# Block sums of the second feed-forward weights: from accumulating DMAs into SBUF at their use to sums made in DRAM during the attention stages

## The chip, the cores and the metric

The kernel runs on one core of one Trainium2 chip. The metric is the device time of one execution in microseconds; the kernel before has a median of 865.25 us in 3 runs (865.21 to 866.35). Engine names are those of the profile: PE is the matrix engine (PEld its weight loads), DVE VectorE, ACT ScalarE, POOL GpSimd, SP SyncE. DMAs issued by SyncE go to hardware queue q1, those of ScalarE to q10, those of GpSimd to the software queue q0; all three are served by the core's 16 DMA engines.

## The reference

One encoder layer on 512 rows of width 1024, in float32: a row norm, one wide projection, three attention branches (a gated linear attention, "GLA"; a softmax attention with forget gates, "FoX"; a cross attention into 256 memory rows), a gated merge with an output projection, and a feed-forward layer with squared ReLU. The part that the change touches:

```python
u2 = rmsnorm(h, g_ffn[l])
h = h + jnp.square(jax.nn.relu(u2 @ w_ff1[l])) @ w_ff2[l]
return rmsnorm(h, g_final)
```

w_ff1 is 1024 x 4096, w_ff2 4096 x 1024.

## The kernel before

All matrix products on weights are made of three products of a high and a low part (hi x hi, lo x hi, hi x lo; `mm3`, lines 122 to 125), so each weight chunk of 128 x 1024 float32 (512 KiB) that arrives from DRAM is split into two: ScalarE casts the high part, VectorE subtracts (`split_w`, lines 112 to 117, and `split`, lines 174 to 176). All weights lie in one DRAM array `wst`, laid out chunk by chunk in the order of use (`chunk_list`). `load_w` (line 109) issues a chunk's load on SyncE into one of three buffers "raw"; its two halves go into one of three buffers "hi" and "lo". So at most three chunks are split ahead of PE and three more loaded ahead of that.

The order of the program is: the front (memory keys and values, the row norms, u); chunk "G" (the low-rank and forget projections), the first fq and fk chunk, four fv chunks, the second fq and fk chunk; then three weaves, in which `weave` (line 160) takes attention steps from a list and puts chunks of projections between them by a count of units: the FoX heads (24 steps, with the gk, gq, fq, fk, gv and gg chunks between), the memory attention (16 steps) and the GLA (20 steps). After them come the last branch, the output projection, and the feed-forward layer.

PE's instructions stand in the order of the source. Those of the other engines, SyncE's and GpSimd's among them, are ordered by a scheduler when the program is built; the order on each engine is then fixed, and an instruction that waits holds up all behind it on its engine.

The feed-forward layer works on four quarters q of the inner width. For each, eight chunks of w_ff1 give the squared activations, and `second(q)` (line 950) multiplies by the quarter's part of w_ff2 by Strassen's scheme in the Winograd form: seven products n of half-size blocks in place of eight. The weights' blocks "11", "21", "12", "22" (two chunks i of 512 KiB each, one after the other in `wst`) are laid out such that the four sums which the scheme needs are plain sums: n = 5 uses 11+12, n = 6 11+12+22, n = 7 12+22, n = 4 the sum of all four. The kernel before loads the eight chunks of a quarter into eight buffers of their own by SyncE (line 954), and makes a sum in place by an accumulating DMA on GpSimd's queue, which adds another chunk from DRAM to the buffer (`factor`, line 961): 8 per quarter, 32 in all. Each chunk of a factor is then split (`split_b`), and 12 products follow.

Of the kernel before, what the change touches and what calls it, by code (L numbers as in the profile page):

```python
# [9 lines left out]
F32 = mybir.dt.float32  # L10
# [4 lines left out]
ALU = mybir.AluOpType  # L15
AX = mybir.AxisListType

P = 128
# [43 lines left out]
def hybrid_block(ctx, tc, chunks, wst, xT, memT, xN, cols, gffn, gfin, wup, cst, out):  # L62
    nc = tc.nc
    PSUM = bass.MemoryType.PSUM
    index = {c: i for i, c in enumerate(chunks)}
# [3 lines left out]
    def nm(s):  # L69
        uid[0] += 1  # L70
        return f"{s}_{uid[0]}"
# [5 lines left out]
    dram = ctx.enter_context(tc.tile_pool(name="dram", bufs=1, space=bass.MemoryType.DRAM))  # L77
# [4 lines left out]
    def mmt(shape=None):  # L82
        return pmm.tile(shape or [P, 512], F32, tag="mm", name=nm("mm"))

    def at_(shape=None):
        return pa.tile(shape or [P, 512], F32, tag="a", name=nm("a"))
# [35 lines left out]
    def mm3(ps, lh, ll, rh, rl, start, stop):  # L122
        nc.tensor.matmul(ps, lh, rh, start=start, stop=False)  # L123
        nc.tensor.matmul(ps, lh, rl, start=False, stop=False)  # L124
        nc.tensor.matmul(ps, ll, rh, start=False, stop=stop)  # L125
# [29 lines left out]
    def run(*gens):  # L155
        for g in gens:
            for _ in g:
                pass

    def weave(steps, units, *gens):  # L160

        fill = chain(*gens)
        done = 0
        for i, st in enumerate(steps):
            st()
            due = units * (i + 1) // len(steps)
            while done < due and next(fill, fill) is not fill:
                done += 1
        run(fill)
# [4 lines left out]
    def split(hi, lo, src):  # L174
        nc.scalar.copy(hi, src)  # L175
        return nc.vector.tensor_tensor(lo, src, f(hi), op=ALU.subtract).ins  # L176
# [174 lines left out]
    with pool("fox") as xp:  # L351
# [176 lines left out]
        for h in range(10):  # L528
            for fn, i in ((fox_values, h - 2), (fox_turn, h - 1), (fox_scores, h)):
                if 0 <= i < 8:  # L530
                    steps.append(partial(fn, i))
        weave(steps, 128, gla_k(0), gla_k(1), gla_q(0), gla_q(1), fox_pair(2), fox_pair(3), gvg,
              *[gla_g(j) for j in range(4)])

# [44 lines left out]
    with pool("mematt") as ap:  # L579
# [52 lines left out]
        for h in range(6):  # L632
            for fn, i in ((mem_values, h - 2), (mem_turn, h - 1), (lambda i: run(mem_q(i)), h + 1), (mem_scores, h)):
                if 0 <= i < 4:
                    steps.append(partial(fn, i))
        weave(steps, 96, branch("gate_fox", "w_fox_o", ofh, ofl, 0))
    kvst.close()
    ofst.close()


    with pool("gla") as lp:
# [5 lines left out]
        for e in range(2):  # L647
            b = slice(64 - 64 * e, 128 - 64 * e)
# [108 lines left out]
        def idle(_):  # L757
# [4 lines left out]
            (decays, 1), (gla_turn, 0), (gla_turn, 1), (key_turn, 1), (gla_scores, 2), (states, 1), (gla_scores, 3),  # L762
            (gla_values, 2), (gla_values, 3), (gla_turn, 2), (gla_turn, 3))]
        weave(steps, 96, branch("gate_mem", "w_mem_o", omh, oml, 1))
    gst.close()
    omst.close()
# [94 lines left out]
    with pool("ff") as yp:  # L861
# [8 lines left out]
        def split_b(raw):  # L870
            split_n[0] += 1
            own = split_n[0] % 4 == 0
            hi, lo = ((yp if own else wp).tile([P, 1024], F32R, tag=g, name=nm(g), bufs=1 if own else 3)
                      for g in (("bhi", "blo") if own else ("hi", "lo")))
            split(hi, lo, raw)
            return [t.rearrange("p (k c) -> p k c", k=2) for t in (hi, lo)]
# [39 lines left out]
        def evac(q, n, t, ps):  # L916
            last = q == NQ - 1
            if n == 1 and last:
                add(C(0, 0, t), ps)
            if n in (6, 7):  # L920
                R = (R6 if n == 6 else R7)[t]
                if q == 0:
                    nc.scalar.copy(R, ps)
                else:
                    add(R, ps)
            if n == 6 and last:
                E, G = R6[t], scratch()
                nc.vector.tensor_tensor(E, held[1][t], R6[t], op=ALU.subtract)
                nc.vector.tensor_tensor(G, held[5][t], E, op=ALU.subtract)
                add(C(1, 0, t), E)  # L930
                add(C(1, 1, t), G)
                add(C(0, 1, t), G)
            if n == 7 and last:
                add(C(1, 1, t), R7[t], ALU.subtract)
                finish(2 + t, 1, 0)
                add(C(1, 0, t), R7[t])
            if n == 4:
                add(C(1, 0, t), ps)
                if last:
                    finish(2 + t, 0, 1)  # L940
            if n == 3:
                add(C(0, 1, t), ps)
                if last:
                    finish(t, 1, 1)
            if n == 2:
                add(C(0, 0, t), ps)
                if last:
                    finish(t, 0, 0)

        def second(q):  # L950
            raw = {(b, i): yp.tile([P, 1024], F32, tag=f"b{b}{i}", name=nm("raw")) for b in ("11", "21", "12", "22")
                   for i in range(2)}
            for (b, i), t in raw.items():
                nc.sync.dma_start(t, wst[index["B", q, i, b]])

            def factor(n, i):

                to, x = {1: ("11", None), 5: ("11", "12"), 6: ("11", "22"), 7: ("12", "22"), 4: ("11", "21"), 3: ("22", None),
                         2: ("21", None)}[n]
                if x is not None:  # L960
                    nc.gpsimd.dma_start(raw[to, i], wst[index["B", q, i, x]], accum_op=ALU.add)  # L961
                return split_b(raw[to, i])

            for n, slot in ((1, 0), (2, 1), (5, 3), (6, 4), (7, 5), (4, 2), (3, 6)):
                keep = n in (1, 5)
                if not keep:
                    ps = [mmt() for _ in range(2)]
                else:
                    ps = held.setdefault(n, [at_() for _ in range(2)] if q == 0 else None)
                end = q == NQ - 1 and n == 3  # L970
                steps = [[0, 1]] if end else [[0], [1]]
                for js in steps:
                    w = {i: factor(n, i) for i in js}
                    for t in range(2):
                        for i in js:
                            for k in range(2):
                                p = 2 * i + k
                                sl = slice(t * P, (t + 1) * P)
                                mm3(ps[t], A[p][0][:, slot, sl], A[p][1][:, slot, sl], w[i][0][:, k, :], w[i][1][:, k, :],
                                    p == 0 and not (keep and q), p == 3 and (not keep or q == NQ - 1))  # L980
                        if js[-1] == 1 and not (keep and q < NQ - 1):
                            evac(q, n, t, ps[t])

        for q in range(NQ):
            A.clear()
            for j in range(8):
                if q == 0 and j < 2:
                    act_evac(first[j])
                    continue
                key = ("T", "w_ff1", P * (8 * q + j))  # L990
                if q == 0 and j < 4:
                    with tc.issue_after(norm_end):
                        w = get_w(key)
                else:
                    w = get_w(key)
                run(gT(w, u2h, u2l, act_evac))
            if q == NQ - 1:
                gl = hp.tile([P, D], F32, tag="gf", name="gl")
                nc.sync.dma_start(gl, gfin)
            second(q)  # L1000
# [60 lines left out]
def build(chunks, arrays):  # L1061
    import concourse.bacc as bacc

    nc = bacc.Bacc("TRN2", target_bir_lowering=False, num_devices=1)
    args = [nc.dram_tensor(f"in_{n}_dram", a.shape, mybir.dt.from_np(a.dtype), kind="ExternalInput").ap()
            for n, a in arrays.items()]
    out = nc.dram_tensor("out_0_dram", (S, D), F32, kind="ExternalOutput").ap()
    with tile.TileContext(nc, schedule_with_timeline_sim=True) as tc:
        with tc.manual_schedule(engines={mybir.EngineType.PE}):
            hybrid_block(tc, chunks, *args, out)  # L1070
    return nc
# [9 lines left out]
```

## Time and profile before

| | us |
|---|---|
| median of 3 runs | 865.25 |
| the profiled execution | 863.63 |
| its span from first to last instruction | 861.9 |
| PE busy | 843.2 |
| VectorE busy | 497.2 |
| ScalarE busy | 406.6 |
| GpSimd busy | 82.0 |

The span is 1.7 us shorter than the profiled execution's time, and that execution is 1.6 us under the median. Matmuls are pipelined, so PE's busy time is no measure of its peak; what matters is where it has no work, and whom it waits for there. An instruction's group is named by its line, engine, operation and operands (out<-in).

### The profile page before, as it was taken

The page shows a single profiled execution, that of the slowest core. Times are in us where ns is not written, and L with a number is a line of the kernel's source. Part 1 is how long each engine was busy: PE and PEld are TensorE (multiplying, and loading weights), DVE is VectorE, ACT ScalarE, POOL GpSimd, SP SyncE. Part 2 cuts the span into 40 slices and gives each one's busy share as a digit, 9 for nine tenths or more (in the row PEclk, how much of TensorE's full clock was granted, in tenths as well). Part 3 has the DMA queues.
Part 4 walks back from the last instruction along what each step waited for, and adds up shares of the span by engine and source line. Part 5 has one row for each costly group of instructions (what it writes and reads, how often), then busy time and mean ns, then how long its engine had stood idle before and what let it go on. Part 6 is the DMA issues. An engine that isn't in the chain of part 4 may idle for free.

```text
span 861.9 us, 10680 instructions
## 1 busy us (share of the span) xinstructions
PE 843.2 (98%) x4081; PEld 696.3 (81%) x4081; DVE 497.2 (58%) x822; ACT 406.6 (47%) x644; POOL 82.0 (10%) x90
## 2 busy tenths in 40 slices
PE   7999999999999999999999999999999999999994
PEld 5778788888888888787888889888888888888883
DVE  5784656756444556474533546655556645655687
ACT  8764746754332432322333434644554355435643
POOL 5100000000000011211112100111001000110011
PEclk9999999999999999999999999999999999999998
DMA  8333321222222122124222413969436924781152
GB/s 324 141 122 99 110 95 65 98 74 74 74 98 96 51 98 74 50 74 172 98 98 98 170 49 127 314 122 233 157 98 127 283 103 98 174 241 50 25 98 97
DMA packets 31074, 104.53 MB, mean 121 GB/s; under 512 B 3728, under 2 KB 4528, under 8 KB 31024
## 3 DMA queue, kind: packets, MB, share of 16 engines
q1 hardware_dynamic: 24624, 83.92, 27.2%
q0 software_dynamic: 4608, 16.78, 11.0%
q10 hardware_dynamic: 1792, 3.16, 1.1%
q8 instruction: 32, 0.52, 0.2%
q14 instruction: 18, 0.15, 0.1%
HBM read 101.73 MB, written 2.11 MB: 120 GB/s over the span
## 4 chain that ended last, share of the span: by engine, by line
PE 91%; DVE 4%; ACT 2%; issue 1%; DMA 1%; SPq 0%; POOL 0%; ACTq 0%; DVEq 0%; POOLq 0%
PE mm L123 25%; PE mm L124 25%; PE mm L125 24%; PE a L123 3%; PE a L125 3%; PE a L124 3%; DVE h L914 1%; PE a L720 1%; DMA raw<-in_wst_dram 1%; PE a L449 1%; PE a L737 1%; PE a L480 1%; PE a L479 1%; PE a L731 1%; PE a L447 1%
## 5 line engine op out<-in xcount | busy, mean ns | idle before, releaser
L116 DVE TENSOR_TENSOR wlo<-raw,whi 128x1024 fp32r<-128x1024 f32 x104 | 131.1, 1264 | 140.1 <-ACT whi L115 138.5
L115 ACT CAST whi<-raw 128x1024 fp32r<-128x1024 f32 x104 | 109.6, 1054 | 169.6 <-PE mm L124 130.5
L123 PE MATMUL mm<-uhi,whi 128*128 128x512 f32 x360 | 142.5, 396 | 0.0
L124 PE MATMUL mm<-ulo,whi 128*128 128x512 f32 x360 | 140.7, 391 | 1.4 <-DVE ulo L176 1.4
L125 PE MATMUL mm<-uhi,wlo 128*128 128x512 f32 x360 | 140.5, 390 | 0.0
L123 PE MATMUL mm<-u2h,whi 128*128 128x512 f32 x240 | 93.4, 389 | 0.0
L124 PE MATMUL mm<-u2l,whi 128*128 128x512 f32 x240 | 93.4, 389 | 0.0
L125 PE MATMUL mm<-u2h,wlo 128*128 128x512 f32 x240 | 93.4, 389 | 0.0
L124 PEld LDWEIGHTS mm<-ulo,whi 128*128 128x128 f32 x360 | 67.7, 188 | 15.8 <-DVE ulo L176 2.9
L125 PEld LDWEIGHTS mm<-uhi,wlo 128*128 128x128 f32 x360 | 67.6, 188 | 14.6 <-DVE wlo L116 0.4
L176 DVE TENSOR_TENSOR lo<-raw,hi 128x1024 fp32r<-128x1024 f32 x42 | 51.2, 1224 | 48.6 <-ACT hi L175 48.1
L123 PEld LDWEIGHTS mm<-uhi,whi 128*128 128x128 f32 x360 | 67.7, 188 | 13.5 <-issue 0.7
L175 ACT CAST hi<-raw 128x1024 fp32r<-128x1024 f32 x42 | 44.1, 1054 | 62.3 <-PE mm L124 23.4
L961 POOL DMA_DIRECT2D raw<-in_wst_dram x32 | 28.1, 879 | 277.1 <-DVE lo L176 201.5
L125 PEld LDWEIGHTS mm<-u2h,wlo 128*128 128x128 f32 x240 | 45.1, 188 | 9.4
L123 PEld LDWEIGHTS mm<-u2h,whi 128*128 128x128 f32 x240 | 45.1, 188 | 9.3
L124 PEld LDWEIGHTS mm<-u2l,whi 128*128 128x128 f32 x240 | 45.1, 188 | 9.2
L123 PE MATMUL mm<-hi,ch 128*128 128x512 f32 x120 | 46.7, 389 | 0.0
L124 PE MATMUL mm<-lo,ch 128*128 128x512 f32 x120 | 46.7, 389 | 0.0
L125 PE MATMUL mm<-hi,cl 128*128 128x512 f32 x120 | 46.7, 389 | 0.0
L571 POOL TENSOR_TENSOR acc<-acc,th 128x512 f32<-128x512 f32 x16 | 24.1, 1504 | 102.7 <-DVE th L570 102.7
L176 DVE TENSOR_TENSOR cl<-ss,ch 128x1024 fp32r<-128x1024 f32 x16 | 19.6, 1225 | 13.4 <-ACT ch L175 13.4
(317 smaller groups left out, 1618.5 us busy)
## 6 DMA issues: line engine op xcount, KB each, us to landing
raw<-in_wst_dram SPq DMA_DIRECT2D x144, 512.0 KB, 3.3
raw<-in_wst_dram POOLq DMA_DIRECT2D x32, 512.0 KB, 5.3
xr<-in_xT_dram SPq DMA_DIRECT2D x4, 512.0 KB, 8.1
nFb<-dF ACTq DMA_DIRECT2D x8, 256.0 KB, 3.3
h<-in_xN_dram SPq DMA_DIRECT2D x4, 512.0 KB, 7.9
memr<-in_memT_dram SPq DMA_DIRECT2D x4, 256.0 KB, 4.6
out_dram<-h ACTq DMA_DIRECT2D x4, 256.0 KB, 2.5
out_dram<-h SPq DMA_DIRECT2D x4, 256.0 KB, 3.0
```

What stands on the lines that cost most here:

```text
L115: nc.scalar.copy(hi, raw)
L116: nc.vector.tensor_tensor(lo, raw, f(hi), op=ALU.subtract)
L123: nc.tensor.matmul(ps, lh, rh, start=start, stop=False)
L124: nc.tensor.matmul(ps, lh, rl, start=False, stop=False)
L125: nc.tensor.matmul(ps, ll, rh, start=False, stop=stop)
L175: nc.scalar.copy(hi, src)
L176: return nc.vector.tensor_tensor(lo, src, f(hi), op=ALU.subtract).ins
L447: nc.tensor.matmul(ps[:, :w], q, K[e][:, 0, :w], start=True, stop=False)
L449: nc.tensor.matmul(ps[:, :w], q, K[e][:, 1, :w], start=False, stop=True)
L479: nc.tensor.matmul(po[:, q0:], vv, PTh[:, c0:c0 + w], start=n == 0, stop=False)
L571: nc.gpsimd.tensor_tensor(acc[j], acc[j], th, op=ALU.add)
L961: nc.gpsimd.dma_start(raw[to, i], wst[index["B", q, i, x]], accum_op=ALU.add)
```

## The change

Sixteen blocks of 1 MiB, T1 to T4 for each quarter, are set up in DRAM. T1 = 11+12, T3 = 12+22, T2 = T1+22, T4 = T2+21. Each is made of a copy from DRAM to DRAM issued by SyncE (line 172 of the changed kernel) and an accumulating DMA from DRAM to DRAM issued by GpSimd (line 170): 16 copies and 16 accumulations, all of 1 MiB. `weave` issues one pair or one operation after each of its steps, in the order of the rounds; with 32 of them they fall, in the source, beside the FoX and memory attention. `second` now loads each factor's chunk directly, from `wst` or from a T block (line 977), into one of six buffers that take turns; the eight buffers and the 32 accumulations there go.

```diff
+    Tsum = {(n, q): dram.tile([2, P, 1024], F32, name=f"T{n}_{q}") for n in (1, 2, 3, 4) for q in range(4)}
+
+    def block(q, b):
+        i = index["B", q, 0, b]
+        return wst[i:i + 2]
+
+    def sum_ops():
+        def op(to, src, add):
+            if add:
+                nc.gpsimd.dma_start(to, src, accum_op=ALU.add, max_dma_last_dim=8192)
+            else:
+                nc.sync.dma_start(to, src)
+
+        for rounds in (((1, "11", 0), (3, "12", 0)), ((1, "12", 1), (3, "22", 1)), ((2, 1, 0),), ((2, "22", 1),), ((4, 2, 0),),
+                       ((4, "21", 1),)):
+            for q in range(4):
+                for n, src, add in rounds:
+                    yield partial(op, Tsum[n, q], block(q, src) if isinstance(src, str) else Tsum[src, q], add)
+
+    sums = sum_ops()
+
     def weave(steps, units, *gens):
...
         for i, st in enumerate(steps):
             st()
+            next(sums, lambda: None)()
...
         def second(q):
-            raw = {(b, i): yp.tile([P, 1024], F32, tag=f"b{b}{i}", name=nm("raw")) for b in ("11", "21", "12", "22")
-                   for i in range(2)}
-            for (b, i), t in raw.items():
-                nc.sync.dma_start(t, wst[index["B", q, i, b]])
-
             def factor(n, i):
 
-                to, x = {1: ("11", None), 5: ("11", "12"), 6: ("11", "22"), 7: ("12", "22"), 4: ("11", "21"), 3: ("22", None),
-                         2: ("21", None)}[n]
-                if x is not None:
-                    nc.gpsimd.dma_start(raw[to, i], wst[index["B", q, i, x]], accum_op=ALU.add)
-                return split_b(raw[to, i])
+                raw = yp.tile([P, 1024], F32, tag="braw", name=nm("raw"), bufs=6)
+                nc.sync.dma_start(raw, {1: block(q, "11"), 2: block(q, "21"), 3: block(q, "22"), 5: Tsum[1, q], 6: Tsum[2, q],
+                                        7: Tsum[3, q], 4: Tsum[4, q]}[n][i])
+                return split_b(raw)
```

The built order, at three places. First SyncE's queue in the front, before the change. All rows are loads of weight chunks; raw_64 and raw_67 are the last two of the memory values, raw_70 is G, raw_77 and raw_82 the first fq and fk chunk.

```order
L109 DMA raw_64_466<-in_wst_dram 128x1024
L109 DMA raw_67_484<-in_wst_dram 128x1024
L109 DMA raw_70_509<-in_wst_dram 128x1024
L109 DMA raw_77_556<-in_wst_dram 128x1024
L109 DMA raw_82_610<-in_wst_dram 128x1024
```

The same place after the change (T1_0 is T1 of quarter 0; L172 rows are the copies of 1 MiB):

```order
L172 DMA T1_0_76<-in_wst_dram 16x16384
L109 DMA raw_64_482<-in_wst_dram 128x1024
L172 DMA T3_0_84<-in_wst_dram 16x16384
L172 DMA T1_1_77<-in_wst_dram 16x16384
L109 DMA raw_67_500<-in_wst_dram 128x1024
L172 DMA T3_1_85<-in_wst_dram 16x16384
L172 DMA T1_2_78<-in_wst_dram 16x16384
L172 DMA T3_2_86<-in_wst_dram 16x16384
L172 DMA T1_3_79<-in_wst_dram 16x16384
L172 DMA T3_3_87<-in_wst_dram 16x16384
L109 DMA raw_70_525<-in_wst_dram 128x1024
L109 DMA raw_77_572<-in_wst_dram 128x1024
```

The first eight copies, which wait for nothing but a free DMA semaphore, stand ahead of G's load. Second, the continuation after the change, up to the load of the second fk chunk (raw_116); raw_94 to raw_105 are the four fv chunks, raw_111 is the second fq chunk.

```order
L109 DMA raw_82_626<-in_wst_dram 128x1024
L109 DMA raw_94_691<-in_wst_dram 128x1024
L172 DMA T2_0_80<-T1_0_76 16x16384
L109 DMA raw_97_721<-in_wst_dram 128x1024
L172 DMA T2_1_81<-T1_1_77 16x16384
L109 DMA raw_102_768<-in_wst_dram 128x1024
L172 DMA T2_2_82<-T1_2_78 16x16384
L172 DMA T2_3_83<-T1_3_79 16x16384
L109 DMA raw_105_798<-in_wst_dram 128x1024
L109 DMA raw_111_839<-in_wst_dram 128x1024
L109 DMA raw_116_877<-in_wst_dram 128x1024
```

Four more copies stand among these loads, and each waits until its T1 block has been summed; the copy into T2_3 so waits for the seventh accumulation in GpSimd's order. The last four copies (T4) follow among the gk and gq chunks: T4_0 ahead of the first gk chunk, T4_1 behind the second, T4_2 and T4_3 between the first gq chunk and the second. Third, GpSimd's queue in the front, after the change; L226 and L360 are the rows that were there before (the powers of the row norms, and the two products of u that GpSimd makes, k = 2 and 5), L170 the accumulations.

```order
L170 DMA T1_0_76<-in_wst_dram 128x2048
L226 TENSOR_TENSOR rr_47_409<-ms_46_408,cst_s_71 128x4
L170 DMA T3_0_84<-in_wst_dram 128x2048
L170 DMA T1_1_77<-in_wst_dram 128x2048
L360 TENSOR_TENSOR ut_58_455<-xr_133,rxb_131 128x512
L170 DMA T3_1_85<-in_wst_dram 128x2048
L360 TENSOR_TENSOR ut_61_467<-xr_133,rxb_131 128x512
L170 DMA T1_2_78<-in_wst_dram 128x2048
L170 DMA T3_2_86<-in_wst_dram 128x2048
```

The three computing rows stood together there before; now one, three and four accumulations stand ahead of them, each of which waits for its copy. The rest of GpSimd's accumulations follow before its next computing row, which belongs to the GLA weave. PE's rows are the same before and after.

## The prediction

> **What bounds the kernel now.** I began with the page: the engines' shares and the digits of the DMA engines over time.
>
> ```profile
> PE 843.2 (98%) x4081; PEld 696.3 (81%) x4081; DVE 497.2 (58%) x822; ACT 406.6 (47%) x644; POOL 82.0 (10%) x90
> ...
> DMA  8333321222222122124222413969436924781152
> ```
>
> TensorE is busy 98% of the span; the DMA engines have most of theirs free. An average can hide a stage that stalls, so next came the table by stretches (columns: length; busy time and count on PE, weight loads, VectorE, ScalarE, GpSimd; clock; DMA share; GB/s).
>
> ```profile
> 38.00:93.00 55.00, 53.62 (x234) 42.70 (x233) 34.62 (x59) 31.04 (x48) 2.09 (x3) 1.00 0.35 115
> 93.00:250.00 157.00, 156.68 (x790) 129.68 (x789) 91.46 (x219) 86.85 (x172) 0.00 (x0) 1.00 0.23 78
> ...
> 541.00:850.00 309.00, 309.00 (x1365) 255.95 (x1364) 188.44 (x246) 156.62 (x202) 28.13 (x32) 1.00 0.55 145
> ```
>
> The last row is the feed-forward stage, where the removed accumulating DMAs run: PE is busy 309.00 of 309.00 us. Its waits in the whole program are these, longest first:
>
> ```profile
> PE mm L125 <- DVE lo L256: 2.7, 5, 1.0
> PE mm L124 <- DVE ulo L176: 1.4, 3, 0.8
> PE a L266 <- POOL wz L263: 1.3, 1, 1.3
> ```
>
> All stand before 46 us, none on a feed-forward block. So **no microsecond of the end hangs on the accumulations that go away**, and the question is what the new DMAs do to the loads of the early stages. Where PE needs them is in its timeline (start, length, line, operands):
>
> ```profile
> 38.85 0.39 PE L123 MATMUL mm<-uhi,whi 128*128 128x512 f32 x1
> ...
> 87.58 0.39 PE L123 MATMUL mm<-uhi,whi 128*128 128x512 f32 x1
> ...
> 117.39 0.39 PE L123 MATMUL mm<-uhi,whi 128*128 128x512 f32 x1
> ```
>
> These are the first products of chunk G (38.85), of the second fk chunk (87.58, the last before the weave) and of the second gq chunk (117.39).
>
> **What goes.** 32 accumulations on GpSimd's queue (q0) and the 32 half-MiB loads of "11" to "22" by SyncE (q1); in their place q1 makes 56 half-MiB loads, each a single one per block. The prices are the queues' rows (packets, MB, share of 16 engines over the span):
>
> ```profile
> q1 hardware_dynamic: 24624, 83.92, 27.2%
> q0 software_dynamic: 4608, 16.78, 11.0%
> ```
>
> q1: 0.272 x 861.9 = 234.4 us for 80.0 MiB, **2.9 us of all 16 engines per MiB**, 1.46 per chunk. q0: 0.110 x 861.9 = 94.8 us for 16 MiB, **5.9 us per MiB** accumulated. So the feed-forward stage loses 95 us of DMA time and gains 24 x 1.46 = 35, and its share sinks from 0.55 to about 0.36. PE waits there for nothing now: gain 0. The six turning buffers let a load go out six blocks ahead; a block is 12 products of 0.227 us (those of the timeline follow each other so), so 16 us against 3.3 to land (row below): cost 0, and if that cover failed, at most the few us of one load per block. GpSimd's 28.13 us of issuing go too, for nothing, as no product waits for it.
>
> **What comes, and where.** 16 copies of 1 MiB on q1 and 16 accumulations of 1 MiB on q0, in DRAM. The source puts them beside the weave's steps; the built order puts the first eight copies far earlier, ahead of G's load, and four more ahead of the load that fk's second chunk needs. I take it that q1's transfers are carried out in order of issue (a rival below drops that). Until when the front's own loads fill the engines is in the digits of 22.5 to 40 us (0.44 us each):
>
> ```profile
> DMA  9972100000019997589410008896000000027984
> ```
>
> They are done at about 24.1. From there, what stands before G is 8 copies and G itself. **A copy's price** no row shows. It must read its bytes, which a load shows at 2.9, and no less, since the engines stand at 9 tenths while loading; the other end is 5.9, if reading and writing DRAM took turns as the two operands of an accumulation do. I take 2.9: a copy is one stream, as a load is. After the data come the tail of landing and the split into two halves:
>
> ```profile
> raw<-in_wst_dram SPq DMA_DIRECT2D x144, 512.0 KB, 3.3
> ...
> L116 DVE TENSOR_TENSOR wlo<-raw,whi 128x1024 fp32r<-128x1024 f32 x104 | 131.1, 1264 | 140.1 <-ACT whi L115 138.5
> L115 ACT CAST whi<-raw 128x1024 fp32r<-128x1024 f32 x104 | 109.6, 1054 | 169.6 <-PE mm L124 130.5
> ```
>
> 3.3 - 1.46 = 1.8 and 1.05 + 1.26 = 2.3, together 4.1. Without a single accumulation G's products start at 24.1 + 8 x 2.9 + 1.5 + 4.1 = 52.9 instead of 38.85: **14 us late at the least**. That SyncE has three raw and three split buffers does not cover it, since the copies stand ahead of the load itself.
>
> The accumulations come on top, and they start as soon as the first copies land. How q0 shares the engines with q1 is seen where both are busy in the feed-forward stage, 587 to 590.5 us:
>
> ```profile
> q0 software_dynamic: 108, 0.44, 69.4%
> q1 hardware_dynamic: 106, 0.43, 33.6%
> ```
>
> 108 packets against 106: they **alternate one for one**, and q0 takes two thirds of the time. A chunk is 128 rows of 4 KB, 8 packets per engine; an accumulation is 128 rows of 8 KB, 8 packets too. So every load that meets a full q0 carries one whole accumulation with it, 5.9 us. I carry the sum to the second fk chunk. After 24.1 stand before it 12 copies and 9 loads (G, fq, fk, four fv, fq, fk). Its 72 load packets and 12 copy packets (one if a 64 KB row is one packet) let 84 of q0's by, 10.5 accumulations:
>
> 24.1 + 12 x 2.9 + 9 x 1.46 + 10.5 x 5.9 + 4.1 = 24.1 + 34.8 + 13.1 + 62.0 + 4.1 = 138.1, against 87.58: **+50.5 us**.
>
> The bounds: the copy of T1 to T2 for the fourth quarter waits for the seventh accumulation, and SyncE with all loads behind it, so n is at least 7 (+30); twelve are there at most (+59). An accumulation into DRAM no row shows either; into SBUF it is 5.9, and if a write to DRAM came as a third turn it would be 5.9 + 2.9 = 8.8 (+30 for 10.5). Less than 5.9 is excluded as long as two operands are read. The copies at 5.9 add 12 x 3.0 = 36.
>
> GpSimd has rows of the front behind its accumulations: the power for the row norms and two products of u (k = 2 and 5). The last of them stands behind an accumulation whose copy is the fourth; that lands before G's load does, so G's start already holds it: 0, and if GpSimd were later than G, the difference.
>
> **In the weave** four copies and what is left of q0 remain. From fk's second chunk to gq's second, PE takes 117.39 - 87.58 = 29.8 us; the four loads and four copies take 5.8 + 11.6, and with one accumulation to a load 23.6, together 41. That is between 0 and 11 more; as the last accumulations wait for copies and do not all fall here, I take 5. After that DMA time is free again (0.23 used), and PE cannot make up what it lost.
>
> Sum: 50.5 + 5 = 55.5 on the profiled execution's 863.63, so 919.1. The median shown is 1.6 above that execution; **I predict 920**.
>
> **Two rules of the Trainium skill.** In "DMA: Bandwidth & Descriptors", section "Latency and other measured facts", the Trainium skill gives copies from HBM to HBM 214 GB/s per direction at full rate. A MiB would take an estimated 4.9 us by it, and the sum would rise by 12 x 2.0 = 24 to 944; no run here shows it. The same page, section "Queues, rings and completion order", lets an engine change queues only after a packet of some 9 to 17 descriptors. By that one copy could let a whole accumulation by instead of one row, n would be 12, and the sum 929; the alternating packets above do not tell the two apart.
>
> **Rivals.** *Cheap accumulations* (only the seven that SyncE must wait for fall before fk): +30 to +36, 893 to 901. For it: accumulations wait for their copies and GpSimd issues in order. Against: at 2.9 a copy three have landed by some 35 us, and a new one lands before an accumulation at 5.9 ends, so q0 is then never empty. *Dear DRAM traffic* (a copy takes up to two turns, 4.6 to 5.9, or an accumulation three, 8.8, or both): 55.5 and 20 to 66 more, 940 to 985. For it: DRAM is touched twice or three times per byte, which no row of before prices. Against: the stores of the output land in no more time than loads of their size:
>
> ```profile
> out_dram<-h ACTq DMA_DIRECT2D x4, 256.0 KB, 2.5
> ```
>
> *Not slower* (the copies don't hold up the loads behind them): from 38 to 250 us the engines have 0.65 x 55 + 0.77 x 157 = 157 us free, and 16 x (2.9 + 5.9) = 141 would fit. If copies ran beside the loads, G would land as before, the end would stand at 863 to 866, and a shorter tail could even make it a little faster. It decides at the point where G's load lands by 38.85 - 2.3 = 36.5: the eight copies would have to take (36.5 - 1.8 - 1.5 - 24.1)/8 = 1.1 us each. Against it: engines at 9 tenths cannot load faster than 2.9 per MiB.
>
> **How the numbers follow.** The forecast (902 to 940) has 0.52, cheap accumulations 0.15, dear traffic 0.28, not slower 0.04, 0.01 for still more. The range takes in the cheap case and most of the dear one: 888 to 970; it leaves out some 0.05 below and 0.12 above. A change under 0.2% could not be told from none here: faster 0.01, same 0.03, slower 0.96.
>
> **What would show it.** Right: in the profile after, PE's wait for the split of G (ulo or wlo) of 14 us or more near 40 us; DMA digits of 9 from the start to beyond 130 us; PE waits before the weave of some 50 us in all; no PE wait and a lower DMA share in the feed-forward stage, its length unchanged. Wrong: G's products at 39 us; or PE waits in the weave's later part, or in the feed-forward stage (the loads of the sums late). The sum's largest unknown is the accumulations' price: 16 MiB on q0 with a share far from 11% of the span would show it.

## The result and the profile after

The changed kernel takes 919.86 us (median of 4 runs, 918.57 to 922.13) where the kernel before takes 865.57 beside it: a ratio of 1.0618, with a 95% interval of 1.0593 to 1.0643. The forecast was 920.0. The profiled execution's span is 918.7 us, 56.8 longer than before. The page of the changed kernel: engines, clock and DMA digits, and the two queues.

```profile
PE 858.1 (93%) x4081; PEld 705.9 (77%) x4081; DVE 499.6 (54%) x822; ACT 407.6 (44%) x644; POOL 68.0 (7%) x74
...
PEclk8958898999999999999999999999999999999998
DMA  9999999722222222222243241454532543452132
...
q1 hardware_dynamic: 28592, 113.28, 34.6%
q0 software_dynamic: 2304, 16.78, 9.1%
```

TensorE does the same 4081 products and sinks from 98% to 93% of a longer span. The DMA digits stand at 9 for seven slices of 23 us, to about 161 us, where before the second to the seventh slice stood at 1 to 3. The table by stretches (columns as in the prediction's) says where the time was lost.

```profile
38.00:93.00 55.00, 27.63 (x94) 20.55 (x92) 22.67 (x37) 18.67 (x32) 6.56 (x9) 0.72 1.02 280
93.00:250.00 157.00, 139.45 (x664) 113.37 (x665) 79.62 (x191) 81.74 (x150) 5.97 (x7) 0.95 0.65 189
...
598.00:907.00 309.00, 309.00 (x1364) 255.84 (x1364) 188.78 (x245) 156.94 (x202) 0.00 (x0) 1.00 0.38 131
```

From 38 to 93 us TensorE now starts 94 products instead of 234, with the DMA engines full. The last row is the feed-forward stage: 309.00 of 309.00 us busy, as before, while its DMA share sank from 0.55 to 0.38. The waits of TensorE in the whole program (total, times, longest):

```profile
PE mm L123 <- ACT whi L115: 35.9, 4, 21.5
PE a L486 <- DVE ri L478: 6.5, 1, 6.5
```

No group of waits came to more than 2.7 before. The four waits on L115 are for the split of a weight chunk: the last chunk of the memory values (3.04), G, the first and the fourth fv chunk. The 6.5 is for the first softmax of the FoX heads. TensorE's timeline has the products that ended these four waits, then the first products of the second fk chunk and of the second gq chunk, which come late without a wait of their own; in brackets the idle time ahead of each and what ended it.

```profile
41.30 0.76 PE L123 MATMUL mm<-whi,mxh 128*128 128x512 f32 x1 [3.04 <-ACT whi L115]
...
69.11 0.80 PE L123 MATMUL mm<-uhi,whi 128*128 128x512 f32 x1 [21.50 <-ACT whi L115]
...
98.32 0.79 PE L123 MATMUL mm<-whi,uhi 128*128 128x512 f32 x1 [7.62 <-ACT whi L115]
...
121.98 0.50 PE L123 MATMUL mm<-whi,uhi 128*128 128x512 f32 x1 [3.76 <-ACT whi L115]
...
135.65 0.39 PE L123 MATMUL mm<-uhi,whi 128*128 128x512 f32 x1
...
174.23 0.39 PE L123 MATMUL mm<-uhi,whi 128*128 128x512 f32 x1
```

G is 30.3 us late, the second fk chunk 48.1, the second gq chunk 56.8: the whole loss is made by then, and nothing behind it gives any back. The DMA packets from 38 to 93 us (packets, MB, share of the 16 engines' time):

```profile
q0 software_dynamic: 905, 6.55, 59.2%
q1 hardware_dynamic: 907, 8.84, 42.6%
```

905 packets of accumulations went beside 907 of loads and copies, and took more of the time than those: the one-for-one turns of the prediction, in the place where it needed them.

### The profile page after: what moved, and what is told of

The parts are those of the page before. It is cut to its first block, busy times and chain, and to the rows that moved or that the text cites. A ratio compares the mean times of both kernels' runs of the same rounds, so it can differ in the third digit from the quotient of the medians.

```text
span 918.7 us, 10678 instructions
## 1 busy us (share of the span) xinstructions
PE 858.1 (93%) x4081; PEld 705.9 (77%) x4081; DVE 499.6 (54%) x822; ACT 407.6 (44%) x644; POOL 68.0 (7%) x74
## 3 DMA queue, kind: packets, MB, share of 16 engines
q1 hardware_dynamic: 28592, 113.28, 34.6%
q0 software_dynamic: 2304, 16.78, 9.1%
## 4 chain that ended last, share of the span: by engine, by line
PE 82%; DMA 12%; DVE 3%; ACT 2%; issue 1%; SPq 0%; POOL 0%; ACTq 0%; DVEq 0%
PE mm L123 22%; PE mm L124 22%; PE mm L125 22%; DMA raw<-in_wst_dram 9%; PE a L124 3%; PE a L125 3%; PE a L123 3%; DMA T<-in_wst_dram 1%; DMA xr<-in_xT_dram 1%; DVE h L937 1%; PE a L743 1%; PE a L502 1%; PE a L760 1%; PE a L472 1%; PE a L503 1%; PE a L754 1%
## 5 line engine op out<-in xcount | busy, mean ns | idle before, releaser
L115 ACT CAST whi<-raw 128x1024 fp32r<-128x1024 f32 x104 | 109.4, 1053 | 210.4 <-PE mm L124 120.2
L123 PE MATMUL mm<-uhi,whi 128*128 128x512 f32 x360 | 144.4, 401 | 21.5 <-ACT whi L115 21.5
L123 PE MATMUL mm<-whi,uhi 128*128 128x512 f32 x64 | 26.8, 418 | 11.4 <-ACT whi L115 11.4
L808 POOL TENSOR_TENSOR rr<-ms,cst_s 128x1 f32<-128x1 f32 x8 | 5.3, 665 | 371.3 <-ACT sq L800 327.2
```

The source lines that it names most:

```text
L115: nc.scalar.copy(hi, raw)
```

## The experiments

The theory from here on is the prediction's: the feed-forward stage had nothing to gain; the copies stand ahead of loads that TensorE waits for; each packet of those queues lets one packet of an accumulation by. Its rivals are that the sheer sum of DMA work costs the time, or that the queue of SyncE does, where a copy waits for a sum and the loads wait behind it.

**1. Only the feed-forward edit (ff_only).** No sums are made; each factor is one load of a block.

```diff
-            next(sums, lambda: None)()
...
-                nc.sync.dma_start(raw, {1: block(q, "11"), 2: block(q, "21"), 3: block(q, "22"), 5: Tsum[1, q], 6: Tsum[2, q],
-                                        7: Tsum[3, q], 4: Tsum[4, q]}[n][i])
+                nc.sync.dma_start(raw, {1: block(q, "11"), 2: block(q, "21"), 3: block(q, "22"), 5: block(q, "12"), 6: block(q, "22"),
+                                        7: block(q, "12"), 4: block(q, "21")}[n][i])
```

> No sums are made: the copies and accumulations are left out, and where the changed kernel loads a sum this one loads one of its blocks (so products 4 to 7 work on other numbers). Theory (the whole loss is made before 165 us by the new DMAs, the feed-forward stage neither gains nor loses): 865.6, within 1.5. Rival (the feed-forward stage has a gain or a loss of its own that hides in the 54 us): 860 or less, or 870 or more.

Measured: 864.93 (12 runs, 863.3 to 866.45) against 864.95, ratio 0.9989 (0.9971 to 1.0008). The 32 accumulations that the change takes out of this stage were worth nothing, and the 24 more loads cost nothing.

**2. Copies without accumulations (copies_only).**

```diff
-                nc.gpsimd.dma_start(to, src, accum_op=ALU.add, max_dma_last_dim=8192)
+                pass
```

> The 16 accumulations are left out, so the T blocks hold plain copies; the copies stand as in the changed kernel, ahead of G's load. Theory (loads queue behind copies, and accumulations share the engines with the loads): G's first product at 24.1 + 8 x 2.43 + 1.3 + 4.1 = 48.9 instead of 69.1, no wait of a chunk after it, 875 to 879. Rival (the copies' place ahead of the loads makes most of the loss, whatever runs beside them): G still later than 60, 895 or more.

Measured: 876.78 (4 runs, 876.39 to 878.16), ratio 1.0120 (1.0086 to 1.0154). G's first product in its timeline, and its largest wait:

```profile
53.05 0.80 PE L123 MATMUL mm<-uhi,whi 128*128 128x512 f32 x1 [8.95 <-ACT whi L115]
```

G comes 14.2 us late, 4.2 later than expected ahead of this run; the prediction's floor without accumulations was 52.9. One long wait, and 12 us in all: the copies make about a fifth of the loss. Their price comes out of the queue rows of this run and of ff_only, which differ by these 16 MiB:

```profile
q1 hardware_dynamic: 28592, 113.28, 37.6%
```

```profile
q1 hardware_dynamic: 28080, 96.50, 33.0%
```

0.376 x 875.1 - 0.330 x 864.6 = 329.0 - 285.3 = 43.7 us of all engines, 2.7 per MiB.

**3. Without the last two rounds (no_t4).** Product 4 loads block "21".

```diff
-        for rounds in (((1, "11", 0), (3, "12", 0)), ((1, "12", 1), (3, "22", 1)), ((2, 1, 0),), ((2, "22", 1),), ((4, 2, 0),),
-                       ((4, "21", 1),)):
+        for rounds in (((1, "11", 0), (3, "12", 0)), ((1, "12", 1), (3, "22", 1)), ((2, 1, 0),), ((2, "22", 1),)):
...
-                                        7: Tsum[3, q], 4: Tsum[4, q]}[n][i])
+                                        7: Tsum[3, q], 4: block(q, "21")}[n][i])
```

> The last two rounds (four copies and four accumulations for T4) are left out, product 4 loads block 21 instead of the sum. Theory (the wait of 6.5 us at 146 us comes from T4's DMAs and the last accumulations beside the load of the forget rows nFb): PE's waits up to the second fk chunk as in the changed kernel (135.6), the one at 146 us gone or nearly, 911 to 914. Rival (that wait is left over from the earlier lateness): 919 to 921.

Measured: 912.53 (4 runs, 911.83 to 913.08), ratio 1.0529 (1.0494 to 1.0564). The second fk chunk starts at 135.59, as in the changed kernel; the first softmax, 6.5 us late there, keeps TensorE waiting 1.9 here.

```profile
PE a L485 <- DVE Pt L478: 1.9, 1, 1.9
```

So the T4 rounds, 8 of the 32 operations, cost some 7 us (1.0618 - 1.0529 of 865), all behind the second fk chunk: the term that the prediction called "in the weave".

**4. Shorter accumulation rows (acc_rows_2k).**

```diff
-                nc.gpsimd.dma_start(to, src, accum_op=ALU.add, max_dma_last_dim=8192)
+                nc.gpsimd.dma_start(to, src, accum_op=ALU.add, max_dma_last_dim=2048)
```

> The accumulations are cut into rows of 2 KB instead of 8 KB; the bytes are the same. Theory (queues take turns packet by packet, so the size of q0's packets sets how long a load of 8 packets takes): a load that meets a full q0 takes about 8 x (0.159 + 0.157) = 2.5 us instead of 6.3, G's first product near 52, the second fk chunk bound by SyncE's wait for the seventh accumulation, 885 to 897. Rival (only the sum of the engines' work counts, not how it is cut): 915 to 921.

Measured: 919.37 (4 runs, 918.12 to 923.19), ratio 1.0616 (1.0576 to 1.0656): no gain, where the theory wanted 23 to 35 us. Yet its first step happened. G's first product moved from 69.11 to 56.76:

```profile
56.76 0.80 PE L123 MATMUL mm<-uhi,whi 128*128 128x512 f32 x1 [9.48 <-ACT whi L115]
```

What took the gain back is in the waits of SyncE's own queue from 60 to 160 us (the waiting line of the kernel, what for, total, times, longest):

```profile
SPq L172 <- DMA T<-in_wst_dram: 73.4, 7, 13.0
```

L172 is a copy; `T<-in_wst_dram` are the transfers into the T blocks that it waits for, accumulations here. With accumulations slowed down by their short rows, the T2 and T4 copies stood 73.4 us at the head of SyncE's queue, and the chunk loads behind them. At 101.22 us the last T2 copy was released and three loads went out right behind it:

```profile
101.22 0.47 SPq L172 DMA_DIRECT2D T<-T  x1
101.79 1.50 SPq L109 DMA_DIRECT2D raw<-in_wst_dram  x3
```

Of the 12.4 us won at G, 8.7 were left at the second fk chunk (126.95) and none at the end. The turns were right, but they were not the only limit. Whether the head of the queue really was the second is run 6.

**5. Longer turns for the accumulations (copy_rows_8k).** The copies' rows of 64 KB become 8 KB, eight rows for one.

```diff
-                nc.sync.dma_start(to, src)
+                nc.sync.dma_start(to, src, max_dma_last_dim=8192)
```

> The copies on SyncE's queue are cut into rows of 8 KB, eight packets for each DMA engine instead of one of 64 KB; bytes, order and the accumulations stay. Theory (the two queues take turns packet by packet, so each packet on SyncE's queue lets one accumulation packet by): all of the early accumulations get in beside the copies and the loads ahead of G, G's first product near 90 to 95 instead of 69.1; the second fk chunk, ahead of which nearly all accumulations stood already, comes 0 to 8 later than 135.6: 920 to 930. Rival (turns go by DMA, or by bytes): G's first product stays within 3 of 69.1 and the time within 918 to 921.

Measured: 930.35 (4 runs, 929.87 to 931.76), ratio 1.0748 (1.0719 to 1.0776). G's first product:

```profile
88.28 0.80 PE L123 MATMUL mm<-uhi,whi 128*128 128x512 f32 x1 [38.78 <-ACT whi L115]
```

19.2 us later than in the changed kernel, though the bytes and the order are the same. The DMA time is nearly so: 9.0% of 930.0 us on q0, as much as there, and 35.4% on q1, 11.3 us more; if all of that is the copies', some 6 us fall to the eight ahead of G. The rest of the 19.2 came with the number of packets, which let more accumulations by ahead of G. The rival, turns by DMA or by bytes, is out. By the Trainium skill ("DMA: Bandwidth & Descriptors", section "Queues, rings and completion order") an engine changes queue only after a packet of about 9 to 17 descriptors; an 8-row share of a copy would then be one turn like a 1-row share, and G would have stayed. The trace does not agree: here each row is a turn. The two smaller steps of the theory were a little off: G came 2 us ahead of the range given, the second fk chunk at 149.43, 13.8 later than in the changed kernel instead of 0 to 8, and the total just above its range.

**6. T2 and T4 copies on GpSimd's queue, with 2 KB rows (split_queue).**

```diff
-        def op(to, src, add):
+        def op(to, src, add, eng):
...
-                nc.gpsimd.dma_start(to, src, accum_op=ALU.add, max_dma_last_dim=8192)
+                nc.gpsimd.dma_start(to, src, accum_op=ALU.add, max_dma_last_dim=2048)
...
-                nc.sync.dma_start(to, src)
+                eng.dma_start(to, src)
...
-                    yield partial(op, Tsum[n, q], block(q, src) if isinstance(src, str) else Tsum[src, q], add)
+                    yield partial(op, Tsum[n, q], block(q, src) if isinstance(src, str) else Tsum[src, q], add,
+                                  nc.sync if isinstance(src, str) else nc.gpsimd)
```

> Accumulation rows of 2 KB, and the copies from one sum to the next (T2 and T4) issued by GpSimd on its own queue, so that no copy on SyncE waits for an accumulation; the copies of blocks (T1 and T3) stay on SyncE ahead of G. Theory (with 2 KB rows alone it was the copy waiting at the head of SyncE's queue, T2 and T4 on accumulations, that held the loads back and kept the time at 919): G's first product near 57, chunk loads issued in one go, waits after fv gone or small: 884 to 890. Rival (SyncE's head waits were not what bound, the sum of packets ahead of the chunks was): 905 or above, with the second fk chunk beyond 120.

Measured: 900.64 (4 runs, 899.64 to 901.6), ratio 1.0405 (1.0374 to 1.0437). 18.7 us better than with short rows alone, and the last copy on SyncE's queue is issued at 28.2 us, so none waits for a sum any more. The head of that queue thus did bind there, and the rival is out; but the time is 11 us above the top of the theory's range. TensorE's waits show what is left:

```profile
PE mm L123 <- ACT whi L115: 21.1, 2, 13.5
PE a L487 <- DVE ri L479: 4.5, 1, 4.5
```

G's start (58.52) is as expected. Not expected were a wait of 7.62 us ahead of the first fv chunk and 4.5 at the first softmax. The same 7.62, to the hundredth, stands ahead of that chunk in the changed kernel and in runs 4, 5 and 9 too, although its first product starts anywhere between 84.8 and 117.3 us in them. A wait that does not move with the loads points away from the DMA. ScalarE's timeline there, in the changed kernel:

```profile
89.44 1.24 ACT L395 ACTIVATE ab<-a 128x264 f32<-128x264 f32 x3
90.71 1.04 ACT L449 CAST K<-K 64x1024 fp32r<-64x1024 f32 x1
...
92.79 1.08 ACT L398 ACTIVATE ab<-ab 128x1056 f32<-128x1056 f32 x1
93.90 1.04 ACT L449 CAST K<-K 64x1024 fp32r<-64x1024 f32 x1
94.96 1.28 ACT L399 ACT_TABLE_LOAD   x1
96.25 1.08 ACT L399 ACTIVATE ab<-ab 128x1056 f32<-128x1056 f32 x1
97.24 1.03 ACT L115 CAST whi<-raw 128x1024 fp32r<-128x1024 f32 x1
```

The chunk, loaded from 70.35 on, had landed at 86.7. Its split (L115, last row) stands in ScalarE's order behind K's casts and the decay logarithms (ab). Before the change it stood well ahead of both. Splits follow the order of the loads; in ScalarE's timeline before the change, the first row here is the split of the first fv chunk, the second that of the third, and the logarithms begin only behind that:

```profile
46.60 1.05 ACT L115 CAST whi<-raw 128x1024 fp32r<-128x1024 f32 x1 [1.31 <-PE mm L124]
...
57.80 1.04 ACT L115 CAST whi<-raw 128x1024 fp32r<-128x1024 f32 x1 [0.72 <-ACT Q L419]
...
60.00 1.20 ACT L372 ACTIVATE ab<-a 128x264 f32<-128x264 f32 x4
```

The built order changed here along with that of the loads. This cost has nothing to do with bytes, so it got two runs of its own.

**7. and 8. The decay logarithms behind the first fv split,** in the changed kernel (after_order) and in split_queue (split_order).

```diff
-        nc.scalar.copy(hi, raw)
+        newest[0] = nc.scalar.copy(hi, raw).ins
...
-        decay_logs()
         fv = v_chunks(OFF["fv"], v_evac)
-        run(islice(fv, 14))
+        next(fv)
+        with tc.issue_after(newest[0]):
+            decay_logs()
+        run(islice(fv, 13))
```

> The changed kernel, but the decay logarithms' instructions on ScalarE stand behind the split of the first fv chunk instead of ahead of it (in the kernel before that split stood ahead of them; in the changed one TensorE waits 8.0 us there while ScalarE works through some 5 us of decay work and 2.7 of K casts, with the chunk landed since 86.7). Theory (that wait is a cost of its own, made by the order and not by the DMA): first fv product near 94 instead of 98.3; the raw buffer of the next load comes free as much earlier, and the time is 914 to 917. Rival (the loads after it bind, so an earlier fv only waits longer for the fq1 chunk): fv earlier all the same, the wait before fq1 longer by as much, and 918.5 to 920.5.

> The run split_queue (accumulation rows of 2 KB, T2 and T4 copies on GpSimd's queue, 900.6) with the decay logarithms on ScalarE behind the split of the first fv chunk. There no chunk is waited for after fv, so theory (the 8.0 us wait before fv is ScalarE's order, and nothing later covers it): first fv product near 82 instead of 86.2, and the time 895 to 897.5. Rival (the wait is the chunk's load after all): 900 to 901.5, fv as late as before.

(The wait that the first text places ahead of fq1 stands ahead of the fourth fv chunk.) Measured: after_order 918.47 (4 runs, 918.35 to 919.59), ratio 1.0620 (1.0603 to 1.0638), 1.4 us under the changed kernel but with no better ratio (1.0618 there), so no gain clear of the noise; split_order 897.51 (5 runs, 897.31 to 898.39), ratio 1.0379 (1.0362 to 1.0395), 3.1 under split_queue and at the upper edge of its range. No run of split_order is as long as one of split_queue, though the intervals of the two ratios overlap. In after_order the first and the fourth fv chunk:

```profile
93.56 0.79 PE L125 MATMUL mm<-whi,uhi 128*128 128x512 f32 x1 [5.92 <-ACT whi L117]
...
121.38 0.80 PE L125 MATMUL mm<-whi,uhi 128*128 128x512 f32 x1 [5.00 <-ACT whi L117]
```

The first is 4.8 us earlier, the fourth only 0.6: its wait grew from 3.76 to 5.00. Its load was issued at 95.5 instead of 99.9 and landed at 120.2 instead of 120.8, since the DMA engines were full in between. So in the changed kernel the order on ScalarE costs next to nothing of its own (the rival); where the loads run less behind, as in split_queue, most of what was won at that place reached the end (83.03 instead of 86.24 at fv, 3.1 at the end). What is left of the wait, 5.9, holds K's casts, which stayed ahead of the split, and the split itself.

**9. T2 and T4 copies on GpSimd's queue, rows of 8 KB (split_8k).** As run 6 without the edit of the accumulations' rows.

> The run split_queue with the accumulations' rows left at 8 KB, so that only the queue of the T2 and T4 copies differs from the changed kernel (919.9). Theory (two separate costs, turns with 8 KB rows and copies that wait at the head of SyncE's queue): G's first product stays near 69, as in the changed kernel, the loads behind it no longer wait for a copy's sums but still share turns with 8 KB rows, second fk chunk at 122 to 132, and 906 to 916. Rival (the queue's head alone made the loss beyond G): 898 to 904. Second rival (with 8 KB rows the turns alone set the loads' pace and the head waits are covered): 917 to 921.

Measured: 926.26 (4 runs, 925.66 to 926.81), ratio 1.0708 (1.0691 to 1.0724): slower than the changed kernel, outside all three ranges. The theory's marks held up to the second fk chunk (G 69.70, fk 130.23), and then came one wait that was in no forecast:

```profile
PE a L487 <- DVE ri L479: 18.4, 1, 18.4
```

TensorE waits for the first softmax. ScalarE's rows ahead of it:

```profile
146.49 1.04 ACT L115 CAST whi<-raw 128x1024 fp32r<-128x1024 f32 x1 [10.04 <-DMA raw<-in_wst_dram]
...
154.85 1.04 ACT L115 CAST whi<-raw 128x1024 fp32r<-128x1024 f32 x1 [3.85 <-DMA raw<-in_wst_dram]
155.92 1.28 ACT L477 ACT_TABLE_LOAD   x1
157.52 0.40 ACT L477 ACTIVATE Pt<-Pt,mx 128x128 f32<-128x128 f32 x1 [0.32 <-DVE mx L475]
```

The softmax (Pt) stands behind the split of a chunk that TensorE does not need yet, and that chunk landed 25 us after its issue. Why so long, the packets from 125 to 160 us say:

```profile
q0 software_dynamic: 591, 7.58, 80.0%
q1 hardware_dynamic: 594, 2.15, 17.7%
```

591 against 594: strict turns again, now with 64 KB rows of copies on q0 as well. The loads got 17.7% of the engines. Row size and queue so work only together: shorter rows alone change nothing in the time (919.4), the other queue alone costs 6.4 (926.3), both together gain 19.2 (900.6).

**10. and 11. The same sums later (late, late_2k).** Each step is queued on SyncE behind the newest chunk load; in late_2k the accumulations' rows are 2 KB as well.

```diff
-        (eng or nc.sync).dma_start(raw, wst[i])
+        newest[0] = (eng or nc.sync).dma_start(raw, wst[i]).ins
...
-            next(sums, lambda: None)()
+            with tc.issue_after(newest[0]):
+                next(sums, lambda: None)()
```

> The same sums of the same blocks, but each step of them is queued on SyncE behind the newest load of a chunk that the weave has asked for, so that the first copy stands behind the second fk chunk instead of ahead of G's load. Theory (the sums cost time only by the packets that they put ahead of the chunk loads which TensorE waits for): G's first product at 39 as before the change, second fk chunk at 87 to 89, then few waits, since the later chunks have slack: 865 to 874. Rival (some 60 MB more of DMA work cost what they cost wherever they stand, because TensorE's early part lives from DMA all through): 890 to 920, with waits in the weave of 25 or more in all. A third case, SyncE's queue held up by a copy that waits for an accumulation: 875 to 890, with chunk loads issued right after an accumulation has landed.

> The same order as the run with late sums, and the accumulations cut into rows of 2 KB instead of 8 KB, so that a chunk's 4 KB packet waits for a shorter one at each turn. Theory (turns by packet): whatever waits are left in the weave with late sums get shorter, 865 to 868, and no longer than the late run. Rival (only the sum of DMA work counts): the same time as the late run.

Measured: late 876.61 (6 runs, 875.33 to 880.34), ratio 1.0133 (1.0105 to 1.0162); late_2k 866.69 (12 runs, 864.43 to 870.58) against 865.3, ratio 1.0012 (0.9992 to 1.0033). All 32 operations are still there; the stretch from 90 to 170 us of late_2k:

```profile
90.00:170.00 80.00, 79.68 (x410) 65.29 (x409) 52.26 (x133) 54.67 (x106) 8.23 (x8) 1.00 1.08 292
```

of late:

```profile
90.00:170.00 80.00, 74.85 (x354) 60.40 (x353) 43.75 (x115) 46.23 (x91) 6.19 (x8) 0.94 0.96 272
```

In late_2k the DMA engines are as full as they can be and TensorE works 79.68 of 80.00 us on 410 products. The kernel before, in the same stretch, does the same with a DMA share of 0.27 instead of 1.08:

```profile
90.00:170.00 80.00, 79.68 (x410) 65.28 (x409) 52.60 (x139) 54.14 (x107) 0.00 (x0) 1.00 0.27 93
```

So the rival that the sum of DMA work costs its time wherever it stands is out. Late without short rows stayed 2.6 us above the theory's range, in the range of its third case. That case's mechanism was not at work: among SyncE's waits of late no copy waits for a sum, and late_2k, which is faster, has one such wait of 11.8 us. Only the length of the rows differs between the two runs, so the length of the turns made the 10 us. Late's longest wait of TensorE (3.1 us, for oT, outputs of the heads) is again vector work behind a late split, as VectorE's rows show:

```profile
125.90 1.23 DVE L118 TENSOR_TENSOR wlo<-raw,whi 128x1024 fp32r<-128x1024 f32 x1 [11.64 <-ACT whi L117]
127.04 0.68 DVE L514 TENSOR_TENSOR oT<-a,th 64x512 f32<-64x512 f32 x1
```

No version beat the kernel before, and run 1 gives no reason to expect one: what the sums relieve is not what binds.

## Why the prediction was right, step by step

**The feed-forward stage gives nothing and costs nothing:** shown by run 1, 0.9989 with an interval that holds 1.

**The copies at 2.9 us per MiB,** chosen from bounds of 2.9 and 5.9: 2.7 in run 2, and in the changed kernel (0.346 x 918.7 - 285.3)/16 = 2.0, so the lower bound itself was a little high. The copies are the same in both, so by this reckoning their price depends on what runs beside them. The Trainium skill's 214 GB/s per direction for copies within HBM ("DMA: Bandwidth & Descriptors", section "Latency and other measured facts"), an estimated 4.9 us per MiB, is not what these copies took. The floor that follows, G at 52.9, was met at 53.05; with 2.7 the same sum gives 51.3, so part of that agreement is luck.

**One-for-one turns:** shown three ways: 905 packets against 907 in the changed kernel, G moved to 56.8 and to 88.3 by the size of rows alone, 591 against 594 in run 9.

**10.5 accumulations of 5.9, together 62.0, ahead of the second fk chunk:** two errors that cancel. Practically all twelve of them were through by then (the twelfth landed at 133.7, the chunk itself at 132.6), and each cost less: 0.091 x 918.7/16 = 5.2 us per MiB by the queue's row. 12 x 5.2 = 62.4. The bound "less than 5.9 is excluded" was wrong by 0.7, and n came out at its upper bound.

The higher n is no failure of the turns but of the count. The prediction took 8 packets of a load and one of a copy on each engine. The queue rows say otherwise: the 24 loads that ff_only makes more than the kernel before are 28080 - 24624 = 3456 packets, 144 each, which is 9 per engine; a copy is (28592 - 28080)/16 = 32, 2 per engine; an accumulation is 2304/16 = 144, again 9. Each transfer has one packet more per engine than it has rows there. Counted so, 9 loads and 12 copies make 105 turns and let 11.7 accumulations by. That the extra packets take a turn like the others is an inference from this agreement.

With the measured prices the sum is 127.7 to 136.1, for a copy of 2.0 to 2.7; the prediction had 138.1. The chunk's split ended at 135.0, and TensorE reached it at 135.65 without a wait, coming from the fourth fv chunk. The forecast is nearer than its terms deserve.

**The weave, +5:** measured 174.23 - 135.65 = 38.6 us where before it took 29.8, so +8.8, and some 7 of it belongs to the T4 rounds by run 3. The size lay in its bounds of 0 and 11; the path was not the one given. The prediction let chunk loads be late for their own products. The longest wait, 6.5 us, is the first softmax: in VectorE's rows the low half of a split ends, and the softmax begins at once,

```profile
149.44 1.23 DVE L116 TENSOR_TENSOR wlo<-raw,whi 128x1024 fp32r<-128x1024 f32 x1 [4.19 <-ACT whi L115]
150.70 0.29 DVE L474 CUSTOM_DVE_ANT_0 Pt<-a,nFb 128x128 f32<-128x128 f32 x1
```

A chunk not yet needed, but split in order ahead of the softmax, passes its lateness on. Run 9 shows the same with 18.4 us.

**SyncE waiting at its queue's head** was used only for a lower bound on n. In the changed kernel one copy waits 10.9 us there for a sum, but this stays hidden, as the next load starts only when the split of the first fv chunk has freed its buffer; in run 4 it set the time. **GpSimd's rows of the front cost 0:** no wait of TensorE names them.

**What the working lacked** is that the order on ScalarE and VectorE also moved: the first fv split went behind the decay logarithms, and on VectorE 15 splits instead of 14 stand ahead of the first softmax. PE's own rows being unchanged, I looked no further than SyncE and GpSimd. At the first place this was covered by the loads (run 7).

**The rivals.** Cheap accumulations (seven ahead of fk) failed, since practically all twelve got by. Dear DRAM traffic failed: both prices came out under mine. "Not slower" needed eight copies at 1.1 us each ahead of G, and they took 2.7; but its remark that the later stages have room for all of it was true, and run 11 puts it there.

The sum of the parts: 48.1 to the second fk chunk and 8.8 in the weave are 56.9, and the spans differ by 56.8. The forecast had 50.5 and 5, the one 2.4 too high and the other 3.8 too low. That the median was met to 0.2 us is luck; that the loss lies where the sum put it, behind copies and one-for-one turns, is not.

**The clock had no term.** The prediction's sign of "some 50 us" of TensorE's waits ahead of the weave came true only in part. The stretch up to the first attention product, before the change and after:

```profile
0.00:93.03 93.03, 85.97 (x418) 68.29 (x418) 58.25 (x92) 59.84 (x103) 15.35 (x20) 1.00 0.48 170
0.00:141.09 141.09, 98.76 (x418) 76.67 (x418) 58.33 (x91) 59.55 (x102) 26.79 (x33) 0.83 1.00 299
```

Of the 48.1 us, 35.3 are added idle time; the other 12.8 are the same 418 products taking longer at a mean clock of 0.83. The forecast counted when loads land, so it got the total without asking how it divides. How much of the 12.8 TensorE would have waited anyway, no run shows.

## What to carry to other kernels

Free DMA time in a profile is worth something only behind the loads that the bottleneck engine waits for: the same 32 transfers cost 54 us ahead of them and under 2 us behind them in short rows (11 in long ones), and what they were to relieve should first be shown to bind. Where two DMA queues are busy, count rows, not bytes: the queue with the longer rows takes the larger share, so a background stream wants short rows on a queue on which no load waits behind it. And when loads move, read the built order of all the engines again: a split, a cast or a softmax that falls behind a late chunk in an in-order engine passes the delay on to work that needed no DMA.

## What the hardware showed besides

The clock granted to TensorE sinks after a stall and stays low for a while after work resumes. The stretches before, in and after G's wait in the changed kernel:

```profile
47.00:69.00 22.00, 0.62 (x2) 0.00 (x0) 7.45 (x16) 5.15 (x10) 3.62 (x6) 0.58 0.97 252
69.00:78.00 9.00, 8.85 (x25) 6.61 (x26) 2.45 (x2) 1.10 (x2) 0.00 (x0) 0.64 1.04 256
78.00:90.00 12.00, 12.00 (x55) 9.96 (x54) 3.52 (x5) 5.08 (x9) 0.00 (x0) 1.00 1.03 284
```

In the 9 us after the wait it makes 25 products at a clock of 0.64, in the 12 us after that 55 at 1.00: some 16 products, 3.6 us, are lost behind one stall. The Trainium skill ("TensorE: Matmul & The Clock Gate", Part 1) describes a gate that halves the clock after an idle window of about 3.4 us and wants at least one busy window of that length to lift it; the trace agrees in kind: 0.64 over 9 us is 6.5 us at half, more than one such window and less than two.

Rows cost time of their own in an accumulation: cut to 2 KB, the 16 MiB of accumulations took 0.102 x 916.4/16 = 5.8 us per MiB instead of 5.2, and run 11 shows the same step (0.098 x 875.1/16 = 5.4 in late, 0.110 x 865.0/16 = 5.9 in late_2k). For copies no such cost is clear: with their rows of 8 KB, q1 took 35.4% of 930.0, 329.2 us, where with rows of 64 KB it took 317.9 in the changed kernel and 329.0 in run 2.
